# Pairs of eight products: the lower right block summed in the fifth product's bank, with differences of activations, and a fifth raw weight tile

## The chip, the core and the metric

The kernel runs on one core of a Trainium2 chip. The metric is device time in microseconds (us), the median of the runs of one program. PE is TensorE (matmul), PEld its weight load, DVE is VectorE, ACT is ScalarE, POOL is GpSimd and SP is SyncE, which here only issues DMAs. Matmuls sum in PSUM, eight banks of 128 x 512 fp32; POOL and DMA work on SBUF.

## What is computed

A decoder trunk of two layers for 256 tokens of width 2048, in fp32. Layer 0 is a gated short convolution, layer 1 an attention without softmax; each is followed by a squared-ReLU MLP with 8192 hidden units. Every sub-layer has a norm before and after. The change is in the MLP, which runs twice:

```python
D_MODEL = 2048; SEQ = 256; D_FF = 4 * D_MODEL

def sq_relu_mlp(u, w_up, w_down):
    return jnp.square(jax.nn.relu(u @ w_up)) @ w_down
...
        u = rmsnorm(h, mlp_pre_g[i])
        h = h + rmsnorm(sq_relu_mlp(u, mlp_w_up[i], mlp_w_down[i]), mlp_post_g[i])
```

## The kernel before

**Precision.** PE multiplies fp32r. Every operand is split into a high part (rounded to fp32r, on ACT) and a low part (the rest, on DVE); a product is three matmuls, high x high, high x low and low x high. Weights come by DMA from SP (`load_one`, L139) into one of `RAW` = 4 raw tiles of 128 x 1024, are split into `whi` (ACT, L163) and `wlo` (DVE, L174), and wait in a ring of 7 split tiles. A raw tile is free for the next load when it has been split.

**The MLP's steps.** The hidden units are cut into 8 steps of 1024, eight up tiles of 128 each. In step e the kernel makes the up tiles of step e+1 (`whole_up`, L944) and uses those of step e for the down projection, in turn: one up tile, then one *pair* (`Down.pair`, L1008), which multiplies two hidden tiles (256 hidden units) by a 256 x 1024 block of the down weights. Four pairs (m = 0 to 3) make one half h of a step, and one half gives one band j of 1024 output columns. `step_chunks` fixes the order of the weights, and PE's order is written out by hand (`manual_schedule` for PE, L89); DVE's, ACT's, POOL's and SP's order in this part is set by the scheduler, with `high_priority` where the code says so.

**An up tile** is 16 matmuls of 128 x 512 (high weights with both parts of the input) and 16 of 128 x 256 (low weights), all in bank 2 (`UP_BANK`). `finish` (L915) has ACT copy the bank's right half (`half`, L917), `Hidden.tile` (L857) has DVE add the left half to it (`s`, L859). After these two the bank is free. ACT applies ReLU and square, and the result is split into the parts of `hid`.

**A pair of seven products** (m = 1, 2, 3 in all steps but the last) is one level of Strassen-Winograd: the 256 x 256 activations and the 256 x 1024 weights are cut into 2 x 2 blocks, and seven block products, 21 matmuls, do instead of eight. Sums and differences of weights are made in `split_seven` (L191, `sums`), those of activations in `sums_of` (L873, `sq`). Products 1, 5, 6 and 7 have banks 6, 7, 0 and 1, tile `more` in the profile; three others go to banks 3, 4 and 5, tile `acc`. All are summed over a *plan* of eight pairs, the second half of one step and the first half of the next with the same band.

**A pair of eight products** (m = 0, and the last step's m = 1 to 3) is the plain block product, 24 matmuls (`eight`, L1036). The upper blocks go to banks 3 and 4, the lower left to bank 5. The lower right has no bank of its own in a plan: it is summed in bank 2 (`own == at`), and is added to its result at once (`add`, L951; DVE at L958, or an ACT copy at L956 the first time).

**At a plan's end** banks 3, 4 and 5 are added to their results, and `add_later` (L962), the *combine*, has ACT copy products 1, 6, 5 and 7 into the buffer `more`; nine accumulating DMAs from POOL (L921) then add them to the four results in SBUF, the last of them chained behind one another. In the last step `add_now` does this on DVE.

So per MLP there are 14 pairs of eight in bank 2's rotation and 42 of seven, the last of them behind the last up tile.

Of the kernel before, what the change touches and what calls it, by code (L numbers as in the profile page):

```python
# [9 lines left out]
F32 = mybir.dt.float32  # L10
# [18 lines left out]
LEAD_UP = 6  # L29
ALONE = 8  # L30
RING = 7
RAW = 4
AHEAD = 4
CALM = 12
UNIT = 1.36
# [51 lines left out]
def trunk(ctx, tc, x, xT, vecs, rows, ws, out):  # L87
# [740 lines left out]
    def result():  # L828
        return res.tile([P, 512], F32, tag="mg", name="mg")[:]
# [4 lines left out]
    def mlp(pool, i, before, after):  # L834
# [5 lines left out]
        def two_parts(parts, src):  # L840
            hi, lo = parts
            nc.scalar.activation(hi, src, AF.Copy)
            nc.vector.tensor_tensor(lo, src, hi.bitcast(F32), op=ALU.subtract)

        class Hidden:


            def __init__(self, e):
                self.xs, self.sums = [None] * (NF // 4), {}
                first, second = SEVEN[e]  # L850
                self.pairs = [2 * m for m in first]
                self.apart = [2 * m for m in first if m not in second]

            def x(self, n, b):
                return [part_of(self.xs, n, b, j) for j in range(2)]

            def tile(self, n, ps, half):  # L857
                s = pool.tile([P, T], F32, tag="s", name="s", bufs=3)
                nc.vector.tensor_tensor(s[:], ps[:, :T], half[:], op=ALU.add)  # L859
# [12 lines left out]

            def sums_of(self, n, x, y):  # L873

# [76 lines left out]
        def add(j, b, c, ps, last=False):  # L951
            r = part[b][2 * j + c]
            with tc.high_priority():
                if r is None:
                    r = part[b][2 * j + c] = result()
                    nc.scalar.activation(r, ps[:], AF.Copy)  # L956
                else:
                    nc.vector.tensor_tensor(r, r, ps[:], op=ALU.add)  # L958
            if last:
                after.post(b, 2 * j + c, r, r, scale[b][:])  # L960

        def add_later(j, p1, p5, p6, p7):  # L962
            t = pool.tile([P, 4, 512], F32, tag="gpost", name="more", bufs=1)
            t1, t5, t6, t7 = (t[:, m, :] for m in range(4))
            for to, ps in ((t1, p1), (t6, p6), (t5, p5), (t7, p7)):
                nc.scalar.activation(to, ps[:], AF.Copy)
            r = {(b, c): part[b][2 * j + c] for b in range(NB) for c in range(2)}
            adds.extend((
                (t6, t1), (r[0, 0], t1), (r[0, 1], t5), (r[1, 0], t7), (r[1, 1], t5),
                (r[0, 1], t6), (r[1, 0], t6), (r[1, 1], t7), (r[1, 1], t6),  # L970
            ))

        def add_now(j, p1, p5, p6, p7):
# [11 lines left out]
        class Down:  # L985


            def __init__(self, j, plan):
                self.j, self.plan, self.ps = j, plan, {}
                sevens_at = [at for at in plan if at[1] in SEVEN[at[0]][at[2]]]  # L990
                whole_at = [at for at in plan if at not in sevens_at and at[0] == STEPS - 1]
                self.range = {at: (at, at) for at in plan if at not in sevens_at}
                for own, ats in (("sum", plan), ("more", sevens_at), ("whole", whole_at)):
                    if ats:
                        self.range[own] = ats[0], ats[-1]

            def products(self, key, own, at, factors):

# [9 lines left out]
            def pair(self, at, first, xs):  # L1008
                e, m, _ = at
                seven = m in SEVEN[e][at[2]]  # L1010
                (self.seven if seven else self.eight)(at, first, xs, 2 * m)
                if "more" in self.range and at == self.range["more"][1]:
                    ps = [self.ps.pop(n) for n in (1, 5, 6, 7)]
                    self.combine = lambda: (add_now if at[0] == STEPS - 1 else add_later)(self.j, *ps)
                    if at != self.plan[-1]:
                        self.combine()
                        self.combine = None
                if at == self.plan[-1]:
                    last = e == STEPS - 1
                    for b, c in sorted(self.ps):  # L1020
                        add(self.j, b, c, self.ps.pop((b, c)), last)
                    if self.combine:
                        self.combine()

            def seven(self, at, first, xs, n):
                b11, b21, b22, t1, t2, t3, t4 = chunk(first)
                s1, s2, s3, s4 = xs.sums[n]
                for key, own, x, w in (
                    (1, "more", xs.x(n, 0), b11), ((0, 0), "sum", xs.x(n + 1, 0), b21), ((0, 1), "sum", s4, b22),
                    (5, "more", s1, t1), (6, "more", s2, t2), (7, "more", s3, t3),  # L1030
                    ((1, 0), "sum", xs.x(n + 1, 1), t4),
                ):
                    self.products(key, own, at, [(x, w)])
                spent(3.5 * UNIT)

            def eight(self, at, first, xs, n):  # L1036
                ws = [chunk(first + t) for t in range(2)]

                def factors(b, c, t):
                    return xs.x(n + t, b), [w[:, c * HALF : (c + 1) * HALF] for w in ws[t]]  # L1040
# [316 lines left out]
```

## Time and profile before

| | us |
|---|---|
| runs | 2152.21, 2153.68, 2164.34; median 2153.68 |
| the profiled execution | 2151.56, of which the span is 2149.4 |
| busy in the span | PE 2121.2, PEld 1804.9, DVE 1708.3, ACT 1386.8, POOL 116.2 |
| granted TensorE clock, mean | 0.997 |
| DMA | 450.28 MB, mean 209 GB/s |

How to read the views: a row of the timeline has start, duration, engine, line, operation, output <- inputs, shape and count, and in brackets the idle time before it and who ended that. A row of the waits has who waited, at which line, for whom, and then total us, times and the longest. A group's row has busy us and mean ns, then idle us before it. Numbers of buffers are left out of names. Ends of matmuls are modelled, since matmuls are pipelined.

### The profile page before, as it was taken

To read this page: it belongs to the slowest core of one execution; us is meant where nothing else is said; L and a number is where in the kernel's file an instruction comes from. 1 tells how busy PE (TensorE), PEld (TensorE's weight loads), DVE (VectorE), ACT (ScalarE), POOL (GpSimd) and SP (SyncE) were. 2 spreads that over 40 slices of the span, in tenths; PEclk is the share of its full clock that TensorE was granted. 3 is DMA by queue.
4 is the path that set the end of the run, shared out by engine and by line. 5 is a ranking of instruction groups with operands and counts; after the bars stand their busy time and mean duration, and the time that the engine had idled before them with its cause. 6 is when DMAs were issued, how large, how long until landed. Compare 5 with 4: busy or idle time off the path is not lost.

```text
span 2149.4 us, 29843 instructions
## 1 busy us (share of the span) xinstructions
PE 2121.2 (99%) x10816; PEld 1804.9 (84%) x10816; DVE 1708.3 (79%) x2525; ACT 1386.8 (65%) x2108; POOL 116.2 (5%) x139
## 2 busy tenths in 40 slices
PE   9999999999999999999999999999999999999998
PEld 8888888888888888888888888889888888888886
DVE  8766655888889888898866777558897888898987
ACT  7545444766666666676567888547666666666664
POOL 0000000010110100101000000000101001011010
PEclk9999999999999999999999999999999999999999
DMA  8655674586876867868574455645867678687684
GB/s 306 214 189 185 192 233 141 196 237 200 248 217 210 236 218 224 239 207 259 170 224 163 157 157 183 211 155 186 230 209 226 213 224 235 204 253 216 206 260 146
DMA packets 132917, 450.28 MB, mean 209 GB/s; under 512 B 14881, under 2 KB 15137, under 8 KB 131745
## 3 DMA queue, kind: packets, MB, share of 16 engines
q1 hardware_dynamic: 113472, 408.65, 58.0%
q0 software_dynamic: 19008, 39.33, 9.4%
q8 instruction: 85, 1.39, 0.3%
q14 instruction: 64, 0.52, 0.1%
q10 hardware_dynamic: 288, 0.39, 0.1%
HBM read 413.19 MB, written 2.10 MB: 193 GB/s over the span
## 4 chain that ended last, share of the span: by engine, by line
PE 84%; DVE 8%; DMA 5%; issue 2%; ACT 1%; SPq 0%; DVEq 0%; ACTq 0%
PE up L905 17%; PE acc L719 11%; PE up L912 9%; PE acc L300 7%; PE acc L301 7%; PE acc L302 7%; DMA raw<-w_mlp 5%; PE more L1004 4%; PE more L1005 3%; PE more L1006 3%; PE acc L1004 3%; PE acc L1005 3%; PE acc L1006 3%; DVE wlo L174 2%; DVE sums L200 2%
## 5 line engine op out<-in xcount | busy, mean ns | idle before, releaser
L174 DVE TENSOR_TENSOR wlo<-raw,whi 128x1024 fp32r<-128x1024 f32 (+1 forms) x506 | 605.4, 1208 | 200.7 <-ACT whi L163 142.8
L163 ACT ACTIVATE whi<-raw 128x1024 fp32r<-128x1024 f32 (+1 forms) x506 | 526.1, 1047 | 243.9 <-PE acc L302 79.7
L905 PE MATMUL up<-u,whi 128*128 128x512 f32 x1952 | 466.8, 390 | 4.7 <-DVE mg L958 4.1
L905 PEld LDWEIGHTS up<-u,whi 128*128 128x128 f32 x1952 | 364.7, 188 | 83.7 <-DVE mg L958 7.5
L912 PEld LDWEIGHTS up<-u,wlo 128*128 128x128 f32 x2048 | 263.6, 191 | 10.3
L912 PE MATMUL up<-u,wlo 128*128 128x256 f32 x2048 | 268.0, 283 | 0.0
L921 POOL DMA_DIRECT2D mg<-more x112 | 100.5, 997 | 1310.6 <-ACT s L860 573.8
L176 DVE SCALAR_TENSOR_TENSOR wlo<-raw,gv,whi 128x512 fp32r<-128x512 f32 (+1 forms) x160 | 132.0, 853 | 42.0 <-ACT whi L163 41.0
L719 PE MATMUL acc<-u,whi 128*128 128x512 f32 x672 | 156.5, 390 | 0.0
L163 ACT ACTIVATE whi<-raw,gv 128x512 fp32r<-128x512 f32 (+1 forms) x160 | 121.8, 801 | 50.7 <-PE acc L302 38.1
L300 PE MATMUL acc<-whi,u 128*128 128x512 f32 x384 | 153.1, 399 | 0.3 <-ACT tk L1194 0.3
L302 PE MATMUL acc<-whi,u 128*128 128x512 f32 x384 | 149.9, 390 | 0.0
L301 PE MATMUL acc<-wlo,u 128*128 128x512 f32 x384 | 149.7, 390 | 0.0
L719 PEld LDWEIGHTS acc<-u,whi 128*128 128x128 f32 x672 | 124.8, 188 | 25.0
L200 DVE TENSOR_TENSOR sums<-raw,sums 128x512 f32<-128x512 f32 x172 | 117.9, 685 | 1.4
L860 ACT ACTIVATE s<-s 128x256 f32<-128x256 f32 x128 | 51.9, 412 | 73.5 <-DVE s L859 72.9
L200 DVE TENSOR_TENSOR sums<-raw,raw 128x512 f32<-128x512 f32 x86 | 59.2, 689 | 48.1 <-DMA raw<-w_mlp 47.5
L917 ACT ACTIVATE half<-up 128x256 f32<-128x256 f32 x128 | 47.5, 378 | 75.4 <-PE up L912 75.3
L302 PEld LDWEIGHTS acc<-whi,u 128*128 128x128 f32 x384 | 72.1, 188 | 15.5
L719 PEld LDWEIGHTS acc<-u,wlo 128*128 128x128 f32 x672 | 83.5, 192 | 1.7
L719 PE MATMUL acc<-u,wlo 128*128 128x256 f32 x672 | 84.2, 283 | 0.0
L300 PEld LDWEIGHTS acc<-whi,u 128*128 128x128 f32 x384 | 72.2, 188 | 14.0 <-ACT tk L1194 0.7
(4467 smaller groups left out, 4073.1 us busy)
## 6 DMA issues: line engine op xcount, KB each, us to landing
raw<-w_mlp SPq DMA_DIRECT2D x512, 512.0 KB, 4.5
raw<-w_in SPq DMA_DIRECT2D x94, 512.0 KB, 4.0
mg<-more POOLq DMA_DIRECT2D x112, 256.0 KB, 7.2
raw<-w_out SPq DMA_DIRECT2D x32, 512.0 KB, 4.2
raw<-w_v SPq DMA_DIRECT2D x32, 512.0 KB, 4.4
raw<-w_k SPq DMA_DIRECT2D x32, 512.0 KB, 4.4
raw<-w_q SPq DMA_DIRECT2D x32, 512.0 KB, 4.3
raw<-w_wo SPq DMA_DIRECT2D x32, 512.0 KB, 3.6
```

The source lines that it names most:

```text
L163: rounded = nc.scalar.activation(hi[:, at], raw[i][:, at], AF.Copy, scale=1.0 if gain is None else gain)
L174: nc.vector.tensor_tensor(lo[:, at], t[:, at], hi[:, at].bitcast(F32), op=ALU.subtract)
L176: nc.vector.scalar_tensor_tensor(lo[:, at], t[:, at], gain, hi[:, at].bitcast(F32), op0=ALU.mult, op1=ALU.subtract)
L200: nc.vector.tensor_tensor(t, x, y, op=ALU.subtract)
L300: nc.tensor.matmul(ps[:], xh, hi[:, a], start=i == 0 and k == 0, stop=False)
L301: nc.tensor.matmul(ps[:], xh, lo[:, a], start=False, stop=False)
L302: nc.tensor.matmul(ps[:], xl, hi[:, a], start=False, stop=i == self.n - 1 and k == self.ks - 1)
L719: nc.tensor.matmul(ps[:, :cols], w, xs[:, :cols], start=k == 0 and part == parts[0], stop=k == KD - 1 and part == parts[1], skip_group_che ...
L905: nc.tensor.matmul(ps, weight(0, first, m), x, start=k == 0, stop=False)
L912: nc.tensor.matmul(pss[n][:, :T], weight(1, first, m), x, start=False, stop=k == KD - 1)
L1004: nc.tensor.matmul(self.ps[key][:], xh, hi, start=first, stop=False)
L1005: nc.tensor.matmul(self.ps[key][:], xh, lo, start=False, stop=False)
```

## The change

- *Lower right block of an eight.* Outside the last step it is summed in product 5's bank (7), whose range over the plan is now called `"fifth"` and begins at the eight. Product 5 is added to both right-hand results at the combine, so the upper right block would get it too; its bank therefore takes (upper - lower activations) x weights instead of upper activations x weights. `Hidden.tile` makes these differences (`dif`, one subtraction on DVE, then a high and a low part) for the two tiles of the coming step's m = 0. The block's own addition to its result is gone, and bank 2 is used by up tiles alone until the last step.
- *Order in an eight*: upper left, lower left, upper right, lower right. Before: upper left, upper right, lower right, lower left.
- *Combine.* Product 5 is copied first. Where the lower right result does not exist yet (the first plan of a band), ACT copies product 5 to it, and one accumulating DMA falls away (4 in the program). The DMAs stand in another order.
- `half` and `s` of every up tile get high priority.
- `RAW` = 5 instead of 4; the DMA scratch of the program is 8192 bytes instead of the default.

```diff
-RAW = 4
+RAW = 5
...
+                self.eights = [2 * m for m in range(4) if m not in first] if e < STEPS - 1 else []
...
-                nc.vector.tensor_tensor(s[:], ps[:, :T], half[:], op=ALU.add)
+                with tc.high_priority():
+                    nc.vector.tensor_tensor(s[:], ps[:, :T], half[:], op=ALU.add)
...
+                elif n - n % 2 in self.eights:
+                    if n % 2 == 0:
+                        self.sums[n] = pool.tile([P, 2, 2, P], F32R, tag="d", name="sums", bufs=2)
+                    parts = [self.sums[n - n % 2][:, n % 2, j, :] for j in range(2)]
+                    d = pool.tile([P, P], F32, tag="dif", name="dif", bufs=1)
+                    nc.vector.tensor_tensor(d[:], s[:, :P], s[:, P:], op=ALU.subtract)
+                    two_parts(parts, d[:])
...
-            copied = nc.scalar.activation(half[:], ps[:, T:], AF.Copy)
+            with tc.high_priority():
+                copied = nc.scalar.activation(half[:], ps[:, T:], AF.Copy)
...
-            for to, ps in ((t1, p1), (t6, p6), (t5, p5), (t7, p7)):
+            evicted = [(t5, p5), (t1, p1), (t6, p6), (t7, p7)]
+            r = {(b, c): part[b][2 * j + c] for b in range(NB) for c in range(2)}
+            if r[1, 1] is None:
+                r[1, 1] = part[1][2 * j + 1] = result()
+                evicted.insert(1, (r[1, 1], p5))
+            else:
+                adds.append((r[1, 1], t5))
+            for to, ps in evicted:
                 nc.scalar.activation(to, ps[:], AF.Copy)
...
-                if "more" in self.range and at == self.range["more"][1]:
+                if at == self.range["fifth"][1]:
...
-                    (5, "more", s1, t1), (6, "more", s2, t2), (7, "more", s3, t3),
+                    (5, "fifth", s1, t1), (6, "more", s2, t2), (7, "more", s3, t3),
...
-                own = "whole" if at[0] == STEPS - 1 else at
-                for c in range(2):
-                    self.products((0, c), "sum", at, [factors(0, c, t) for t in range(2)])
-                self.products((1, 1), own, at, [factors(1, 1, t) for t in range(2)])
-                if own == at:
-                    add(self.j, 1, 1, self.ps.pop((1, 1)))
-                self.products((1, 0), "sum", at, [factors(1, 0, t) for t in range(2)])
+                products((0, 0), "sum", lambda t: xs.x(n + t, 0), 0)
+                products((1, 0), "sum", lambda t: xs.x(n + t, 1), 0)
+                if at[0] == STEPS - 1:
+                    products((0, 1), "sum", lambda t: xs.x(n + t, 0), 1)
+                    products((1, 1), "whole", lambda t: xs.x(n + t, 1), 1)
+                else:
+                    products((0, 1), "sum", lambda t: [xs.sums[n][:, t, j, :] for j in range(2)], 1)
+                    products(5, "fifth", lambda t: xs.x(n + t, 1), 1)
...
-    nc = _bacc.Bacc("TRN2", target_bir_lowering=False, num_devices=1)
+    nc = _bacc.Bacc("TRN2", target_bir_lowering=False, num_devices=1, dynamic_dma_scratch_size=8192)
```

Three places in the order of the instructions. PE, the second half of the eight at step 0, half 1 (numbers are those of buffers and of weight tiles), before:

```order
L1004 MATMUL more_4559<-whi162_4419,hid4_3860 128x512
L1005 MATMUL more_4559<-wlo162_4420,hid4_3860 128x512
L1006 MATMUL more_4559<-whi162_4419,hid4_3860 128x512
L1004 MATMUL more_4559<-whi163_4458,hid4_3860 128x512
L1005 MATMUL more_4559<-wlo163_4459,hid4_3860 128x512
L1006 MATMUL more_4559<-whi163_4458,hid4_3860 128x512
L1004 MATMUL acc_4568<-whi162_4419,hid4_3860 128x512
```

After:

```order
L1023 MATMUL acc_4576<-whi163_4475,sums_3863 128x512
L1021 MATMUL more_4583<-whi162_4434,hid4_3860 128x512
L1022 MATMUL more_4583<-wlo162_4435,hid4_3860 128x512
L1023 MATMUL more_4583<-whi162_4434,hid4_3860 128x512
L1021 MATMUL more_4583<-whi163_4475,hid4_3860 128x512
L1022 MATMUL more_4583<-wlo163_4476,hid4_3860 128x512
L1023 MATMUL more_4583<-whi163_4475,hid4_3860 128x512
L914 MATMUL up_4590<-u4_3406,whi164_4481 128x512 x4
```

The lower right block (`more`) has moved from the third place to the last and into product 5's bank, and the upper right block reads the differences (`sums`).

DVE around the read-out of an up tile (`s`) ahead of an eight behind a combine (step 1, half 1; whi198 and wlo198 belong to the next seven), before:

```order
L174 TENSOR_TENSOR wlo198a_5362<-raw198_5259,whi198a_5361 128x512
L859 TENSOR_TENSOR s_5346<-up_5293,half_5344 128x256
L174 TENSOR_TENSOR wlo198b_5366<-raw199_5298,whi198b_5365 128x1024
L174 TENSOR_TENSOR wlo198t_5370<-sums_5356,whi198t_5369 128x1024
L843 TENSOR_TENSOR hid4_5350<-s_5346,hid4_5350 128x128
L882 TENSOR_TENSOR sq_5463<-s_5346 128x128
L958 TENSOR_TENSOR mg_4145<-mg_4145,more_5395 128x512
L174 TENSOR_TENSOR wlo198u_5374<-sums_5356,whi198u_5373 128x1024
```

After:

```order
L174 TENSOR_TENSOR wlo198a_5384<-raw198_5279,whi198a_5383 128x512
L861 TENSOR_TENSOR s_5368<-up_5315,half_5366 128x256
L174 TENSOR_TENSOR wlo198b_5388<-raw199_5320,whi198b_5387 128x1024
L174 TENSOR_TENSOR wlo198t_5392<-sums_5378,whi198t_5391 128x1024
L843 TENSOR_TENSOR hid4_5372<-s_5368,hid4_5372 128x128
L891 TENSOR_TENSOR sq_5484<-s_5368 128x128
L174 TENSOR_TENSOR wlo198u_5396<-sums_5378,whi198u_5395 128x1024
```

`s` stands between the same two rows; the addition of the block (`mg`) is gone.

ACT at the same place, before:

```order
L208 ACTIVATE whi198a_5361<-raw198_5259 128x512
L208 ACTIVATE whi198b_5365<-raw199_5298 128x1024
L208 ACTIVATE whi198t_5369<-sums_5356 128x1024
L917 ACTIVATE half_5344<-up_5293 128x256
L860 ACTIVATE s_5346<-s_5346 128x256
```

After:

```order
L208 ACTIVATE whi198a_5383<-raw198_5279 128x512
L208 ACTIVATE whi198b_5387<-raw199_5320 128x1024
L927 ACTIVATE half_5366<-up_5315 128x256
L208 ACTIVATE whi198t_5391<-sums_5378 128x1024
L862 ACTIVATE s_5368<-s_5368 128x256
```

`half` stands one weight split earlier.

More of the change, by code (lines that the diff above doesn't have):

```diff
@@ L964, in add_later @@
             t1, t5, t6, t7 = (t[:, m, :] for m in range(4))
-            for to, ps in ((t1, p1), (t6, p6), (t5, p5), (t7, p7)):
+            evicted = [(t5, p5), (t1, p1), (t6, p6), (t7, p7)]
[6 more added lines that the diff above has]
+            for to, ps in evicted:
                 nc.scalar.activation(to, ps[:], AF.Copy)
-            r = {(b, c): part[b][2 * j + c] for b in range(NB) for c in range(2)}
             adds.extend((
-                (t6, t1), (r[0, 0], t1), (r[0, 1], t5), (r[1, 0], t7), (r[1, 1], t5),
-                (r[0, 1], t6), (r[1, 0], t6), (r[1, 1], t7), (r[1, 1], t6),
+                (t6, t1), (r[0, 0], t1), (r[0, 1], t5), (r[1, 0], t7),
+                (r[1, 1], t7), (r[0, 1], t6), (r[1, 0], t6), (r[1, 1], t6),
             ))
@@ L991, in __init__ @@
                 whole_at = [at for at in plan if at not in sevens_at and at[0] == STEPS - 1]
[L992 to L995, printed above, removed]
+                fifth_at = [at for at in plan if at not in whole_at]
+                self.range = {
+                    own: (ats[0], ats[-1])
+                    for own, ats in (("sum", plan), ("more", sevens_at), ("fifth", fifth_at), ("whole", whole_at)) if ats
+                }
             def products(self, key, own, at, factors):
@@ L1037, in eight, with products @@
                 ws = [chunk(first + t) for t in range(2)]
-                def factors(b, c, t):
-                    return xs.x(n + t, b), [w[:, c * HALF : (c + 1) * HALF] for w in ws[t]]
-                own = "whole" if at[0] == STEPS - 1 else at
-                for c in range(2):
-                    self.products((0, c), "sum", at, [factors(0, c, t) for t in range(2)])
-                self.products((1, 1), own, at, [factors(1, 1, t) for t in range(2)])
-                if own == at:
-                    add(self.j, 1, 1, self.ps.pop((1, 1)))
-                self.products((1, 0), "sum", at, [factors(1, 0, t) for t in range(2)])
+                def products(key, own, x, c):
+                    self.products(key, own, at, [
+                        (x(t), [w[:, c * HALF : (c + 1) * HALF] for w in ws[t]]) for t in range(2)
+                    ])
+                products((0, 0), "sum", lambda t: xs.x(n + t, 0), 0)
[6 more added lines that the diff above has]
+                    products(5, "fifth", lambda t: xs.x(n + t, 1), 1)
                 spent(4 * UNIT)
```

## The prediction

> **What bounds the kernel now.** I read the page first, then who waits for whom on PE, then PE's timeline, then DVE's, and the DMA share last.
>
> ```profile
> span 2149.4 us, 29843 instructions
> PE 2121.2 (99%) x10816; PEld 1804.9 (84%) x10816; DVE 1708.3 (79%) x2525; ACT 1386.8 (65%) x2108; POOL 116.2 (5%) x139
> ```
>
> PE sets the time. But 99% is no proof that only 28 us are to be had: a matmul's row lasts 0.39 us while the next starts 0.23 us later (timeline below), so a row's modelled end hides part of each stall. Who PE waits for, first the matmuls and then the weight loads ahead of them:
>
> ```profile
> PE more L1004 <- DVE s L859: 12.9, 12, 2.2
> PE up L905 <- DVE mg L958: 4.1, 7, 0.7
> PE up L905 <- DVE s L859: 0.6, 1, 0.6
> ...
> PEld more L1004 <- DVE s L859: 21.8, 23, 2.7
> PEld up L905 <- DVE mg L958: 7.5, 8, 1.1
> ```
>
> Almost all of PE's waiting in 2.1 ms belongs to one bank, number 2. An up tile is summed in it and read out by DVE (`s`, L859). The eight's lower right block then uses the same bank ("more", L1004) after only 12 matmuls of cover, and the next up tile must wait until DVE has added that block to its result (`mg`, L958). No row has PE waiting for weights in the MLPs.
>
> An eight without a wait, then a seven, in PE's timeline (start, duration):
>
> ```profile
> 501.87 2.08 PE L912 MATMUL up<-u,wlo 128*128 128x256 f32 x16
> 503.79 0.40 PE L1004 MATMUL acc<-whi,hid 128*128 128x512 f32 x1
> 504.02 0.40 PE L1005 MATMUL acc<-wlo,hid 128*128 128x512 f32 x1
> ...
> 509.25 3.79 PE L905 MATMUL up<-u,whi 128*128 128x512 f32 x16
> 512.88 2.08 PE L912 MATMUL up<-u,wlo 128*128 128x256 f32 x16
> ...
> 519.58 3.79 PE L905 MATMUL up<-u,whi 128*128 128x512 f32 x16
> 523.21 2.08 PE L912 MATMUL up<-u,wlo 128*128 128x256 f32 x16
> ```
>
> From one up tile's end to the next one's, an eight takes 514.96 - 503.95 = 11.01 us and a seven 525.29 - 514.96 = 10.33. From an up tile's end to the next one's start there are 509.25 - 503.95 = 5.30 us in an eight (24 matmuls), 519.58 - 514.96 = 4.62 in a seven (21). The worst eight:
>
> ```profile
> 455.73 2.08 PE L912 MATMUL up<-u,wlo 128*128 128x256 f32 x16
> ...
> 460.17 0.39 PE L1006 MATMUL acc<-whi,hid 128*128 128x512 f32 x1
> 462.79 0.50 PE L1004 MATMUL more<-whi,hid 128*128 128x512 f32 x1 [2.23 <-DVE s L859]
> ...
> 464.05 0.62 PE L1006 MATMUL more<-whi,hid 128*128 128x512 f32 x1
> 464.47 0.63 PE L1004 MATMUL acc<-whi,hid 128*128 128x512 f32 x1
> ...
> 467.03 4.02 PE L905 MATMUL up<-u,whi 128*128 128x512 f32 x16
> 470.89 2.08 PE L912 MATMUL up<-u,wlo 128*128 128x256 f32 x16
> ```
>
> The up tile ended at 457.81, the next began at 467.03: 9.22 us, 3.92 over the clean 5.30. All waits together are taken from the ends of the first and last up tiles of each MLP's steps:
>
> ```profile
> 413.83 1.96 PE L912 MATMUL up<-u,wlo 128*128 128x256 f32 x15
> ...
> 1004.80 2.08 PE L912 MATMUL up<-u,wlo 128*128 128x256 f32 x16
> ...
> 1497.80 1.72 PE L912 MATMUL up<-u,wlo 128*128 128x256 f32 x13
> ...
> 2091.40 2.08 PE L912 MATMUL up<-u,wlo 128*128 128x256 f32 x16
> ```
>
> 415.79 to 1006.88 and 1499.52 to 2093.48 are 591.09 + 593.96 = 1185.05 us for 28 eights and 82 sevens. Without a wait they would take 28 x 11.01 + 82 x 10.33 = 1155.34. So **29.7 us** are lost: more than the 17.6 of PE's own wait rows, and what the weight loads' rows (29.3) say.
>
> **The change part by part.** *The bank.* The lower right block goes to product 5's bank 7, as the last product. The next reader of bank 2 is then the next up tile, 24 matmuls after the last one. `s` must end within 5.30 us of its up tile's end instead of 2.6, and the wait for `mg` has nothing left to wait for. The latest `s` of any eight is the one above, on DVE:
>
> ```profile
> 457.63 0.69 DVE L200 TENSOR_TENSOR sums<-raw,raw 128x512 f32<-128x512 f32 x1 [2.78 <-DMA raw<-w_mlp]
> ...
> 462.32 0.41 DVE L859 TENSOR_TENSOR s<-up,half 128x256 f32<-128x256 f32 x1
> ...
> 471.67 0.69 DVE L200 TENSOR_TENSOR sums<-raw,raw 128x512 f32<-128x512 f32 x1 [1.48 <-DMA raw<-w_mlp]
> ...
> 474.74 0.42 DVE L859 TENSOR_TENSOR s<-up,half 128x256 f32<-128x256 f32 x1
> ```
>
> It ended at 462.73, 4.92 us after the tile. That is inside 5.30, so with `s` where it is, every eight's wait goes. Only one seven waits now for more than 0.3 us, 0.6 us by the row above. Taken off: 29.7.
>
> *The clock.* Behind two waits like this PE also ran slower (a stretch, its length, each engine's busy time, then granted clock, DMA share, GB/s):
>
> ```profile
> 464.00:466.00 2.00, 2.00 (x6) 1.57 (x6) 1.41 (x3) 0.61 (x2) 0.87 (x1) 0.51 1.01 275
> ```
>
> The granted clock was 0.51, and from 464.05 matmuls came 0.42 us apart instead of 0.23, about 8 of them: 1.6 us each time, inside the 29.7. I take it to go with the wait. The Trainium skill (TensorE: Matmul & The Clock Gate, "HAM oscillation — how this bites in real kernels") gives as its abstract rule that idle gaps over about 3.4 us bring the half clock. By it a 2.23 us gap could not be the cause, the slow stretch would stay, and the sum would be 3.2 us smaller. The trace has the half clock begin 1.3 us after the gap's end, so I go by the row.
>
> *What is late next.* In the eights just behind a combine (one in each step) `s` is late because DVE stands in `sums` until a raw tile lands. If DVE and DMA do not move, PE arrives earlier and waits at the following seven. In the case above the next tile ended at 472.97 and its `s` at 475.16, 2.19 later. With the tile 3.92 earlier this is 6.11 against a cover of 4.62: 1.5 us given back. The same reckoning at all 28 eights gives more than 0.2 us at four, 1.5, 1.5, 2.0 and 3.0, in all **8.2 us** as the upper bound; the lower is 0. The fifth raw tile works against it: SP issues the same loads in the same order, but each is released one tile sooner, and DVE's idle rows of 2.78 and 1.48 us are the room. Whether it lands sooner is the question, as the engines are full there:
>
> ```profile
> 548.00:550.00 2.00, 1.11 (x6) 0.60 (x5) 2.00 (x4) 0.42 (x1) 1.63 (x2) 1.00 1.14 283
> ```
>
> A load that was requested before the burst of accumulating DMAs need not land inside it, so I lean to the rows with room: 2 us given back.
>
> *Differences of activations.* Added: 28 subtractions and 28 low parts on DVE, 28 roundings on ACT. Removed: 24 DVE additions of the block; four copies on ACT move from the eight to the combine.
>
> ```profile
> L843 DVE TENSOR_TENSOR hid<-s,hid x42: 278/283/293, 408.4 to 2005.8; 128x128 fp32r<-128x128 f32 x42
> L842 ACT ACTIVATE hid<-s x42: 289/295/315, 407.6 to 2003.8; 128x128 fp32r<-128x128 f32 x42
> ...
> L958 DVE TENSOR_TENSOR mg<-mg,more x26: 676/686/689, 508.1 to 2118.5; 128x512 f32<-128x512 f32 x26
> ...
> 420.00:1007.00 587.00, 579.25 (x2941) 491.73 (x2940) 512.38 (x721) 395.56 (x594) 55.97 (x64) 1.00 0.76 226
> ```
>
> DVE: 56 x 0.283 - 24 x 0.686 = -0.6 us. ACT: 28 x 0.295 = 8.3 us over two MLPs, beside 191 us idle in each. Cost on the path 0; the cover is DVE's 75 idle us in each MLP's steps. The differences are made a step ahead of their use.
>
> *Order of the products, banks.* The second product now uses bank 5, emptied last at the end of a plan, and the last one bank 7, emptied by a copy to `more`. On ACT, at the plan's end before the worst eight:
>
> ```profile
> 452.49 0.62 ACT L956 ACTIVATE mg<-acc 128x512 f32<-128x512 f32 x1
> ...
> 453.58 0.63 ACT L966 ACTIVATE more<-more 128x512 f32<-128x512 f32 x1
> ```
>
> Both are free by 454.21. The second product of that eight starts 6 matmuls after 457.6 and the fourth at about 461.7: 4.8 and 7 us of room, cost 0.
>
> *Raised priority* of `half` and `s`. On DVE the order keeps `s` between the same weight rows; on ACT `half` moves ahead of one split. Between -1 and +1 us; I take 0.
>
> *Half the DMA scratch, four accumulating DMAs fewer.* The trace shows no ring. Accumulations land in 7.2 us:
>
> ```profile
> mg<-more POOLq DMA_DIRECT2D x112, 256.0 KB, 7.2
> ```
>
> Their results are read a step, about 83 us, later. Between -0.5 us and the whole of that room; cost 0, since few can be in flight at a time.
>
> **Sum.** 29.7 - 2.0 = 27.7 us. The profiled execution took 2151.56 us (span 2149.4 and 2.2 around it), giving 2123.9. It lies 2.1 under the median of the three runs, 2153.68; for medians I forecast 2153.7 - 27.7 = **2126.0**. One per cent, about what a measurement of this kernel can tell from no change, is 21.5 us.
>
> **Rivals.** *Given back in full.* 29.7 - 8.2 = 21.5, 2132. For it: DMA share 1.14 in the burst. Against it: those idle rows of DVE. Chance 0.13, half of it on each side of one per cent.
>
> *The stretch behind a combine is bound by DMA as a whole*, so that its waits merely move to the sevens: of the 28 eights, the 14 behind a combine hold about 20.6 of the 29.7, and 9 remain: 2145, no change. Against it: after the worst eight, the next `s` came 2.2 us after its tile, not 4.6, so the sevens have room. Chance 0.08.
>
> *Slower: DVE waits in front of* `s`. Raised priority can place `s` so early that DVE stands until `half` is there, with all weight work behind it. Now DVE spends nothing there:
>
> ```profile
> L859 DVE TENSOR_TENSOR s<-up,half 128x256 f32<-128x256 f32 x128 | 52.8, 416 | 0.0
> ```
>
> DVE's spare is about 75 us in 55 up tiles, 1.36 us each. Above that weights fall behind and PE waits: at 1.8 us it is 110 x 0.44 = 48 us, 2174. It decides at 1.36 + 27.7/110 = 1.6 us. Against it: the order has moved `s` by no row at an eight. Chance 0.05.
>
> That the bank wait stays, because `s` moves later by more than the added 2.7 us of cover: 0.02, same.
>
> **How the numbers follow.** My forecast 0.72; the rivals 0.13, 0.08, 0.05, 0.02. Faster by over 1%: 0.72 + half of 0.13 less a little for the forecast's own edge, 0.76. Slower: 0.05. Within: 0.19. The likeliest case alone, with 0 to 5 us given back and 2 us of scatter, spans 2120 to 2131; the range reaches to the first rival with 6 us over it, 2120 to 2138, and leaves out under 2 in 10.
>
> **What would show it.** The wait rows of PE for `s` at the "more" product and for `mg` at the up tile are gone; the summed waits of PE are under 5 us, what is left stands at sevens behind a combine and names `s`. No slice between the start and the end shows a clock under 1. DVE busy is the same within 5 us, ACT about 8 more. The distance from first to last up tile falls from 1185 to about 1157. Wrong would be: new waits of PE for whi, wlo or the sums, idle time in front of `s` on DVE, or POOL's accumulations stretching into the next combine.

## The result, and the profile after

The changed kernel took 2121.39 us (median of 4 runs, 2120.85 to 2121.52), the kernel before, run beside it, 2156.27 (4 runs, 2152.21 to 2164.34). The ratio is 0.9833, 95% interval 0.9802 to 0.9864: faster by 1.7%. The forecast was 2126.0 in a range from 2120 to 2138. The number holds; the experiments show that a good part of the reason given for it does not.

The profiled execution took 2121.52 us. The head of its page:

```profile
span 2119.8 us, 29868 instructions
PE 2109.0 (99%) x10816; PEld 1805.5 (85%) x10816; DVE 1700.5 (80%) x2557; ACT 1389.6 (66%) x2136; POOL 112.6 (5%) x135
...
PE 99%; DMA 0%; DVE 0%; ACT 0%; SPq 0%; issue 0%; DVEq 0%; ACTq 0%
```

The last line is the chain that ended last: PE alone. Before it read PE 84%, DVE 8%, DMA 5%. The span fell by 2149.4 - 2119.8 = 29.6 us. All that PE's matmuls still wait for in the whole program:

```profile
PE warm L709 <- DVE ones L104: 1.1, 1, 1.1
PE lead L719 <- ACT whi L163: 0.7, 1, 0.7
PE tr L253 <- DVE h L480: 0.3, 1, 0.3
```

Bank 2 is gone from the list. The place that was the worst eight, and the seven behind it, in PE's timeline after:

```profile
456.36 2.08 PE L921 MATMUL up<-u,wlo 128*128 128x256 f32 x16
...
463.74 3.79 PE L914 MATMUL up<-u,whi 128*128 128x512 f32 x16
467.37 2.08 PE L921 MATMUL up<-u,wlo 128*128 128x256 f32 x16
...
474.07 3.80 PE L914 MATMUL up<-u,whi 128*128 128x512 f32 x16
```

458.44 to 463.74 is 5.30 us and 469.45 to 474.07 is 4.62, the two clean distances; before, the eight took 9.22. The ends of the first and last up tiles of each MLP's steps:

```profile
414.38 2.08 PE L921 MATMUL up<-u,wlo 128*128 128x256 f32 x16
...
991.88 2.08 PE L921 MATMUL up<-u,wlo 128*128 128x256 f32 x16
...
1484.31 2.08 PE L921 MATMUL up<-u,wlo 128*128 128x256 f32 x16
...
2061.80 2.08 PE L921 MATMUL up<-u,wlo 128*128 128x256 f32 x16
```

416.46 to 993.96 and 1486.39 to 2063.88 are 577.50 + 577.49 = 1154.99 us, 30.1 less than the 1185.05 before and what 28 clean eights and 82 clean sevens take (1155.34). Nothing was given back. The rest of the program is the same within 0.7 us: 492.4 us between the two MLPs' steps (492.6 before), 55.9 behind them (55.9), 0.7 more ahead of them.

So the time came out of the stretch that the prediction named. But another row moved that the prediction's sum does not contain. DVE's wait for raw weight tiles, before and then after:

```profile
DVE sums L200 <- DMA raw<-w_mlp: 63.9, 61, 2.8
```

```profile
DVE sums L200 <- DMA raw<-w_mlp: 17.7, 23, 1.8
```

A change of a bank on PE does not make weights land sooner. This is where the study began.

### The profile page after: what moved, and what is told of

It reads as the page before. It is cut to its first block, busy times and chain, and to the rows that moved or that the text cites. A ratio compares the mean times of both kernels' runs of the same rounds, so it can differ in the third digit from the quotient of the medians.

```text
span 2119.8 us, 29868 instructions
## 1 busy us (share of the span) xinstructions
PE 2109.0 (99%) x10816; PEld 1805.5 (85%) x10816; DVE 1700.5 (80%) x2557; ACT 1389.6 (66%) x2136; POOL 112.6 (5%) x135
## 4 chain that ended last, share of the span: by engine, by line
PE 99%; DMA 0%; DVE 0%; ACT 0%; SPq 0%; issue 0%; DVEq 0%; ACTq 0%
PE up L914 21%; PE up L921 12%; PE acc L719 11%; PE acc L300 8%; PE acc L302 8%; PE acc L301 7%; PE acc L1021 5%; PE acc L1022 5%; PE acc L1023 5%; PE more L1022 4%; PE more L1021 4%; PE more L1023 4%; PE lead L719 1%; PE up L916 1%; PE tr L253 1%; DMA raw<-w_in 0%
## 5 line engine op out<-in xcount | busy, mean ns | idle before, releaser
L921 PEld LDWEIGHTS up<-u,wlo 128*128 128x128 f32 x2048 | 263.6, 191 | 10.3
L301 PEld LDWEIGHTS acc<-wlo,u 128*128 128x128 f32 x384 | 72.3, 188 | 13.4
```

Of the source, the lines that this page charges most:

```text
L301: nc.tensor.matmul(ps[:], xh, lo[:, a], start=False, stop=False)
L921: nc.tensor.matmul(pss[n][:, :T], weight(1, first, m), x, start=False, stop=k == KD - 1)
```

## The experiments

Theory: the gain is bank 2's turn, as predicted. Rival: it is the fifth raw tile, which takes away what makes `s` late. All twelve kernels stand against the kernel before on the same chip.

| run | what differs | us, median (range) | ratio, 95% | DVE's wait for raw tiles, us |
|---|---|---|---|---|
| bank_alone | after, four raw tiles, no priority | 2145.66 (2142.42-2148.11) | 0.9946, 0.9929-0.9964 | 80.1 |
| raw5_only | before, five raw tiles | 2123.28 (2122.63-2123.51) | 0.9843, 0.9829-0.9858 | 12.4 |
| scratch_only | before, half the scratch | 2160.19 (2154.44-2163.59) | 1.0002, 0.9991-1.0012 | 73.7 |
| prio_only | before, raised priority | 2157.94 (2151.39-2163.74) | 1.0002, 0.9988-1.0016 | 67.9 |
| order_only | before, block last | 2170.45 (2169.04-2173.42) | 1.0067, 1.0049-1.0085 | 67.5 |
| no_adds | before, no accumulating DMAs | 2125.42 (2124.56-2125.72) | 0.9850, 0.9835-0.9864 | 14.3 |
| raw5_prio | before, five tiles, priority | 2122.95 (2122.25-2124.49) | 0.9840, 0.9825-0.9855 | 10.7 |
| bank_noprio | after, no priority | 2120.71 (2120.54-2120.78) | 0.9828, 0.9812-0.9845 | 19.3 |
| raw6_only | before, six raw tiles | 2121.88 (2121.57-2122.38) | 0.9834, 0.9820-0.9849 | 3.0 |
| gated_adds | before, accumulations spread | 2161.74 (2158.80-2170.88) | 1.0020, 1.0005-1.0035 | 63.6 |
| bank_gated | bank_alone, accumulations spread | 2134.17 (2131.52-2136.74) | 0.9889, 0.9871-0.9907 | 70.8 |
| bank_late5 | bank_noprio, fifth tile held back at the start | 2120.67 (2120.40-2121.22) | 0.9827, 0.9811-0.9843 | 14.4 |

### The parts of the change, one at a time

**bank_alone** is the changed kernel, with its half scratch, without the fifth raw tile and without the priority:

```diff
-RAW = 5
+RAW = 4
...
-                with tc.high_priority():
-                    nc.vector.tensor_tensor(s[:], ps[:, :T], half[:], op=ALU.add)
+                nc.vector.tensor_tensor(s[:], ps[:, :T], half[:], op=ALU.add)
...
-            with tc.high_priority():
-                copied = nc.scalar.activation(half[:], ps[:, T:], AF.Copy)
+            copied = nc.scalar.activation(half[:], ps[:, T:], AF.Copy)
```

> The changed kernel with four raw tiles again and without the raised priority of half and s: the bank, the differences, the order in the eight and the halved scratch alone. Bank theory: the whole gain lies in taking the lower right block out of the up tiles' bank, so 2121 to 2132 us, the upper end if sevens behind a combine give back the 8.2 us that were reckoned. Rival (the fifth raw tile brings s forward and that is the gain): 2140 or more, with PE waiting for s at up tiles.

It gained 0.5%, not 1.7. All 28 eights are clean at 5.30 us, as the prediction had it. But the wait came back at four sevens. PE's timeline, the next up tile's start at each of them:

```profile
478.10 5.26 PE L913 MATMUL up<-u,whi 128*128 128x512 f32 x16 [3.04 <-DVE s L860]
...
567.45 6.57 PE L913 MATMUL up<-u,whi 128*128 128x512 f32 x16 [3.74 <-DVE s L860]
...
1559.85 5.43 PE L913 MATMUL up<-u,whi 128*128 128x512 f32 x16 [3.25 <-DVE s L860]
...
1648.92 5.27 PE L913 MATMUL up<-u,whi 128*128 128x512 f32 x16 [3.31 <-DVE s L860]
```

The brackets sum to 13.3 us. The groups of 16 matmuls behind them last 5.26 to 6.57 us instead of 3.79, 7.4 us more in all, since the clock is at half there (columns as in the prediction's stretch, the clock third from the end):

```profile
478.00:480.00 2.00, 1.90 (x5) 1.52 (x6) 2.00 (x4) 1.92 (x4) 0.00 (x0) 0.50 0.57 121
```

Together 20.7 us given back of 29.7 (21.5 by the ends of the first and last up tiles), where the prediction had put 8.2 as the upper bound. DVE at the first of the four shows why:

```profile
472.58 0.69 DVE L200 TENSOR_TENSOR sums<-raw 128x512 f32<-128x512 f32 x1 [2.80 <-DMA raw<-w_mlp]
474.56 0.69 DVE L200 TENSOR_TENSOR sums<-raw,raw 128x512 f32<-128x512 f32 x1 [1.28 <-DMA raw<-w_mlp]
...
477.63 0.42 DVE L860 TENSOR_TENSOR s<-up,half 128x256 f32<-128x256 f32 x1
```

The up tile ended at 470.28, its `s` at 478.05: 7.77 us, against 4.62 of cover. My bound had kept DVE where it was, with that `s` ending at 475.16. It was 2.9 us later than that, standing 4.1 us for two raw tiles where it had stood 1.5 for one. Why those tiles came later than in the kernel before is not settled: PE asks earlier, and the order of the copies and accumulations at a combine changed as well. In sum DVE waits 80.1 us, 63.6 to 73.7 in the kernels below that keep four tiles, the old products and the accumulating DMAs. Moving the bank changes who waits for the late `s`, not that it is late.

**raw5_only** is the kernel before with the fifth tile and the smaller scratch that makes room for it:

```diff
-RAW = 4
+RAW = 5
...
-    nc = _bacc.Bacc("TRN2", target_bir_lowering=False, num_devices=1)
+    nc = _bacc.Bacc("TRN2", target_bir_lowering=False, num_devices=1, dynamic_dma_scratch_size=8192)
```

> The kernel before with five raw tiles (and the halved scratch that makes room). Bank theory: bank 2 still changes hands twice in each eight; waits for s shrink by what DVE idles in front of raw tiles there, waits for mg stay at about 6 us: 2140 to 2154 us. Rival (raw tile): in the changed kernel s ends within 2.1 us of its tile at every eight, inside even the old cover of 2.6 us; if that is the raw tile's doing, the waits for s go here too and 2125 to 2133 us come out.

2123.28 us, 36.0 under the kernel before on its chip: one number gives what the whole change gave (34.9 against the runs beside it; the best version, below, 37.3), with bank 2 used as before and 12 matmuls of cover. DVE at the place of the worst eight (before: a wait of 2.78 us, then `s` at 462.32):

```profile
455.43 1.41 DVE L200 TENSOR_TENSOR sums<-raw,sums 128x512 f32<-128x512 f32 x2
...
460.76 0.42 DVE L859 TENSOR_TENSOR s<-up,half 128x256 f32<-128x256 f32 x1
```

From these sums to `s` DVE works without a wait, and `s` ends 2.7 us after its tile (456.36 + 2.08 in this kernel too) instead of 4.9. What is left of bank 2's waits in the whole program is on the weight loads:

```profile
PEld more L1004 <- DVE s L859: 1.7, 4, 0.5
```

The theory falls here. The bank was where the lateness showed, and the fifth tile takes the lateness away.

**scratch_only**, since every run with five tiles also has the smaller scratch:

```diff
-    nc = _bacc.Bacc("TRN2", target_bir_lowering=False, num_devices=1)
+    nc = _bacc.Bacc("TRN2", target_bir_lowering=False, num_devices=1, dynamic_dma_scratch_size=8192)
```

> The kernel before with the DMA scratch halved to 8192 bytes and nothing else: four raw tiles, the old products, no raised priority. The fifth raw tile needs this smaller scratch to fit, so every run with five tiles had both; this run has the scratch alone. Theory (the gain of the fifth raw tile is the tile's): no difference, 2156 us with a ratio of 0.998 to 1.002, DVE's wait for raw tiles of the MLPs 60 to 70 us, PE's matmul waits for bank 2 at the lower right block 10 to 20 us. Rival (the smaller scratch changes how accumulating DMAs and loads share the engines, and so makes part of the gain): under 2145 us, DVE's wait under 45 us. Slower by the scratch (too few places for nine accumulations in flight): over 2165 us, accumulations landing later than 7.2 us.

No difference, 1.0002, and the accumulations land as before, median 7.4 us (7.2). So raw5_only's gain is the tile's. DVE's wait of 73.7 us beside 63.9 in a kernel of the same time also says how far that row scatters with four tiles.

**prio_only** raises the priority in the kernel before:

```diff
-                nc.vector.tensor_tensor(s[:], ps[:, :T], half[:], op=ALU.add)
+                with tc.high_priority():
+                    nc.vector.tensor_tensor(s[:], ps[:, :T], half[:], op=ALU.add)
...
-            copied = nc.scalar.activation(half[:], ps[:, T:], AF.Copy)
+            with tc.high_priority():
+                copied = nc.scalar.activation(half[:], ps[:, T:], AF.Copy)
```

> The kernel before with high priority for half and s, nothing else. Bank theory: s stays behind the sums that wait for a raw tile, so little moves: 2146 to 2156 us. Rival (priority): s moves ahead of them, waits for s go: 2125 to 2135 us.

Nothing: 1.0002, and bank 2's waits are there as before (18.6 us of matmuls for `s`, 4.5 for `mg`).

**order_only** puts the lower right block last in each eight of the kernel before, still in bank 2:

```diff
+                self.products((1, 0), "sum", at, [factors(1, 0, t) for t in range(2)])
                 self.products((1, 1), own, at, [factors(1, 1, t) for t in range(2)])
                 if own == at:
                     add(self.j, 1, 1, self.ps.pop((1, 1)))
-                self.products((1, 0), "sum", at, [factors(1, 0, t) for t in range(2)])
```

> The kernel before with the lower right block as the last of the eight's products, still in bank 2. s then has 18 matmuls of cover, about 3.9 us, and only three eights have a later one: waits for s fall from some 22 us to under 3. But the block's addition has no cover: DVE's 0.68 us and what stands in front of it on DVE, 0.9 to 1.5 us at each of 28 eights, 25 to 42 us of waits for mg at the up tile. Bank theory (both hand-overs count): 2155 to 2172 us. Rival (only the lateness of s counts): 2130 to 2136 us.

Slower by 0.7%. PE's waits show the trade:

```profile
PE up L905 <- DVE mg L958: 24.7, 24, 2.0
...
PE more L1004 <- DVE s L859: 4.8, 5, 1.3
PE up L905 <- ACT mg L956: 3.9, 4, 1.0
```

The wait for `s` shrinks to 4.8 us, but the block's own addition now has no matmuls over it, and each of the 28 eights waits about one microsecond for it. The new order is good only together with the other bank.

### What makes the raw tiles late

**no_adds** leaves the accumulating DMAs out of the kernel before, so four products are missing from the results:

```diff
-            for a, more in adds[:3]:
-                with tc.issue_after(copied.ins):
-                    nc.gpsimd.dma_start(a, more, accum_op=ALU.add)
             del adds[:3]
```

> The kernel before with four raw tiles and all as it was, but the 126 accumulating DMAs behind the combines are left out, so products 1, 5, 6 and 7 are missing from the results of these plans; only its time is of interest. Raw-tile theory (a load that has to pass through the burst of accumulating DMAs lands too late, DVE stands in front of it, s comes late, PE waits for bank 2): DVE's wait of 64 us for raw tiles falls under 20, PE's waits under 5, 2120 to 2130 us. Rival (four raw tiles are too few at any time, burst or not): DVE's wait stays over 40 us and 2140 or more comes out.

2125.42 us, nearly what the fifth tile gives. The same two stretches behind the combine at 456 us, first without the accumulations:

```profile
456.00:458.00 2.00, 2.00 (x17) 1.96 (x16) 2.00 (x3) 2.00 (x4) 0.00 (x0) 1.00 0.00 0
458.00:460.00 2.00, 2.00 (x10) 1.63 (x10) 2.00 (x4) 0.73 (x2) 0.00 (x0) 1.00 0.44 49
```

and then in the kernel before:

```profile
456.00:458.00 2.00, 2.00 (x18) 1.96 (x17) 0.37 (x1) 0.94 (x3) 0.00 (x0) 1.00 1.10 215
458.00:460.00 2.00, 2.00 (x11) 1.63 (x10) 2.00 (x4) 1.73 (x3) 0.00 (x0) 1.00 1.14 205
```

The third pair is DVE's busy time, the last but one number the DMA share. Without accumulations the DMA engines have run out of free tiles to fill (share 0.00) and DVE works all the time. With them the engines are full, and DVE, which works in its order, stands in `sums` with `s` behind it: 0.37 us busy out of 2. The changed kernel in the same place:

```profile
456.00:458.00 2.00, 2.00 (x17) 1.92 (x16) 1.97 (x3) 2.00 (x4) 1.38 (x2) 1.00 1.13 221
458.00:460.00 2.00, 2.00 (x12) 1.70 (x11) 2.00 (x4) 1.92 (x3) 0.00 (x0) 1.00 1.12 202
```

Its DMA engines are as full (1.13, 1.12) and DVE does not wait, because the tiles that it needs were asked for earlier. A seven uses four tiles in 10.33 us, one each 2.58. So with four tiles a load has about 10.3 us from its buffer's release to the release of the next one in that place, with five 12.9 (an estimate from those rows). Loads land no faster with five: between 400 and 1010 us the median is 4.6 us against 4.5 and the longest 10.7 against 8.9. They start one tile sooner.

**raw6_only** goes one further:

```diff
-RAW = 4
+RAW = 6
...
-    nc = _bacc.Bacc("TRN2", target_bir_lowering=False, num_devices=1)
+    nc = _bacc.Bacc("TRN2", target_bir_lowering=False, num_devices=1, dynamic_dma_scratch_size=8192)
```

> The kernel before with six raw tiles. Raw-tile theory: with five, DVE waits 12 us for raw tiles and PE for 1.7 us in loading weights; the sixth can only take off what is left, at most 2 us, and starts one more load into the crowded beginning, where five already cost about 0.6 us: 2121.5 to 2124 us. If lateness of raw tiles still cost more than the waits show: under 2121.

```profile
DVE sums L200 <- DMA raw<-w_mlp: 3.0, 5, 0.8
```

DVE's wait goes from 12.4 us to 3.0, and the time by 1.4 us, from 2123.28 to 2121.88, though on another chip; in the traces the distance from first to last up tile goes from 1156.4 to 1156.0. Little more is to be had from tiles, since PE hardly waits.

**gated_adds** keeps four tiles and spreads a combine's accumulations: up to three are issued when each up tile has been read, by a small copy on POOL.

```diff
+            if adds:
+                gate = small("gate", bufs=2)
+                seen = nc.gpsimd.tensor_copy(gate[:], half[:, :1])
             for a, more in adds[:3]:
-                with tc.issue_after(copied.ins):
+                with tc.issue_after(seen.ins):
```

> The kernel before with four raw tiles and all accumulating DMAs kept, but three at a time: a one-column copy of half on POOL stands ahead of each three, so they wait for an up tile's end and come in three groups some 10 us apart instead of as fast as their chain allows. Raw-tile theory: the burst is what makes raw tiles late, so DVE's wait for them falls from 64 us to 15 to 40, and the time to 2121 to 2140 us. Rival (what counts is the accumulations' total traffic beside four tiles, not the burst): DVE's wait stays at 60 or more and 2148 to 2160 comes out.

No gain, 1.0020. At 456 us DVE is now busy for all of both stretches, but its waits in the program sum to 63.6 us as before, and PE's to this:

```profile
PE more L1007 <- DVE s L859: 20.2, 12, 2.4
...
PE up L905 <- DVE s L859: 5.2, 9, 1.2
```

The wait has moved to later tiles. So it is not the burst as such: beside four tiles the same accumulations cost as much when they are spread in this way. **bank_gated** does the same to bank_alone (with the same lines):

```diff
-RAW = 5
+RAW = 4
...
-                with tc.issue_after(copied.ins):
+                with tc.issue_after(seen.ins):
```

> The bank's change with four raw tiles and no raised priority (2145.7 before this), with the accumulating DMAs gated in the same way. Raw-tile theory: the four waits at sevens behind a combine go with the burst: 2120 to 2128 us. Rival: they stay, 2140 or more.

2134.17, between the two forecasts. That is 11.5 us better than bank_alone (on another chip), though DVE waits almost as long (70.8 us against 80.1). PE now has nine short waits and no slow clock:

```profile
PE up L913 <- DVE s L860: 7.2, 9, 1.5
```

Together with the longer cover the spread helps, because none of the waits gets long; the mean granted clock is 0.999, in bank_alone 0.995. Against gated_adds, on the same chip, the bank's change is worth 27.6 us here (2161.74 to 2134.17). That points to how the lateness is spread: the latest `s` ends 8.5 us after its up tile in bank_alone and 6.2 in bank_gated, where the cover of a seven is 4.62. Which of the delays the spread shortens was not tested further.

### What the bank and the priority add to five tiles

**raw5_prio** is raw5_only with the two lines of prio_only, and **bank_noprio** the changed kernel without them:

```diff
-RAW = 4
+RAW = 5
...
+                with tc.high_priority():
...
```

> The kernel before with five raw tiles and raised priority, without the bank's change. Five tiles alone gave 2123.3, the whole change 2121.4. If the bank makes these 1.9 us: 2122.5 to 2124. If the priority makes them: 2121.0 to 2121.8.

```diff
-                with tc.high_priority():
-                    nc.vector.tensor_tensor(s[:], ps[:, :T], half[:], op=ALU.add)
+                nc.vector.tensor_tensor(s[:], ps[:, :T], half[:], op=ALU.add)
...
```

> The changed kernel without the raised priority: five raw tiles and the bank. If the bank makes the last 1.9 us: 2121.0 to 2121.8. If the priority makes them: 2122.5 to 2124.

2122.95 and 2120.71, on one chip. Against raw5_only and the changed kernel, which were measured apart from them, the priority is worth 0.3 us in one pair and costs 0.7 in the other: nothing that can be told. The bank, beside five tiles, is worth 1.6 us with the priority (2122.95 to 2121.39) and 2.6 without (2123.28 to 2120.71). The ranges of the runs don't touch, but neither pair was measured side by side. The traces agree on a size: from first to last up tile raw5_only and raw5_prio take 1156.4 us, the changed kernel and bank_noprio 1155.0. So it is there, at about 1.4 us, under 0.1%.

**bank_late5** asks if a fifth load in the first microseconds costs anything; the fifth tile is held until the first weights are split:

```diff
+    spare = wpool.tile([P, CW], F32, tag="raw", name="spare")
...
+        if i == 0:
+            nc.vector.tensor_copy(spare[:, :1], lo[:, CW - 1 :].bitcast(F32))
```

> The changed kernel without raised priority (2120.7) whose fifth raw tile is held back at the start until the first weight tile has been split, as with four tiles, by one column copied into it on DVE. If the fifth tile's early load is what delays PE's first steps (PE reached the MLP's first eight 0.65 us later than before the change): 2119.8 to 2120.4 us. If not: 2120.5 to 2121.0.

2120.67 against 2120.71: no. In the traces the first up tile of the MLP's steps ends at 415.62 us, without the hold at 415.70. These two are the fastest versions measured, 0.03% under the changed kernel and measured apart from it, so not told apart from it.

## Why the prediction was right, and where it was wrong

*The bank.* The size was right in the traces: 29.7 us forecast for the waits, 30.1 measured from first to last up tile. The cause was not. "So with `s` where it is, every eight's wait goes" is what bank_alone shows, but beside five tiles the new bank is worth 1.6 to 2.6 us, and without them a net 0.5%. The same waits can be taken away from two sides, by more cover over a late `s` or by an earlier `s`; the sum counted them once and put them down to the first. The fifth tile does the second, for 28.7 of the 30.1 us in the traces (1185.05 to 1156.4). Whatever clears these waits ends near the same time, so neither the number nor the signs that the prediction had named could tell the cause: raw5_only too has PE's waits for bank 2 gone, but for the 1.7 us of weight loads, and a distance near 1157.

*The level.* By medians the change is worth 34.9 us, against 27.7 forecast. The execution of the kernel before that was profiled, 2151.56 us, was a fast one: the medians of that kernel lie at 2156.27 to 2159.33, and the traces of scratch_only and prio_only, kernels of the same time, lose 38.5 and 36.0 us between first and last up tile where this one loses 29.7. Of the 4.6 us between 2126.0 and 2121.39, 2.0 are the give-back that did not come, and 2.1 were added for a difference between execution and median that the changed kernel, free of the wait, does not have. Nothing hangs on it that the eight read as the worst, 9.22 us, has one of 9.29 beside it in the second MLP.

*What is late next* is the step that failed. It took 2.0 us, with 8.2 as the upper bound. In the changed kernel it is 0; without the fifth tile it is 20.7. Two things were wrong in it. The bound held DVE and DMA still while PE moved forward, but DVE's stand for raw tiles grew. And it left out the slow clock behind the waits, 7.4 of the 20.7 us, though the prediction had that cost in its own sum. The four sevens of bank_alone are the four that it had reckoned. The right question was in it, as "whether it lands sooner"; the answer, that the fifth tile decides the whole case, got 6 us of weight. DVE in the changed kernel shows how near it was at the seven of 469.45:

```profile
467.97 0.69 DVE L200 TENSOR_TENSOR sums<-raw 128x512 f32<-128x512 f32 x1 [1.26 <-DMA raw<-w_mlp]
470.34 0.69 DVE L200 TENSOR_TENSOR sums<-raw,raw 128x512 f32<-128x512 f32 x1 [1.68 <-DMA raw<-w_mlp]
...
473.41 0.42 DVE L861 TENSOR_TENSOR s<-up,half 128x256 f32<-128x256 f32 x1
```

`s` ended at 473.83, 4.38 us after its tile, with 4.62 of cover. The changed kernel clears its worst seven by 0.24 us.

*The clock* went with the waits, as said. The mean is 0.999 after and was 0.997; the stretch from 464 to 466 us, at 0.51 before, is at 1.00. The sign named for it, no slice of the page under 1, says nothing: every slice reads 9 tenths before and after.

*Differences of activations.* The rows hold: 28 subtractions and 28 low parts at 0.284 us are 16.0, the 24 additions gone were 16.4. The page's busy time of DVE fell by 7.8 us all the same, outside the 5 that I had allowed, and ACT's rose by 2.8 instead of 8. The page counts time in which two instructions overlap once, and the short ones start 0.20 us apart while lasting 0.28. Counted like this from the two traces, the new rows add 11.4 us and the additions gone take off 14.7, which is 3.3 of the 7.8. The other 4.5 us are older rows, the `sums` of raw tiles above all, that last as long as before and overlap more with those ahead of them. None of it lay on the path.

*Order of the products, banks:* cost 0, as forecast; PE waits for neither bank 5 nor 7. order_only shows what it would have cost without the other bank.

*Raised priority:* 0 taken, within 0.7 us of 0 measured. The slower rival's mechanism is in the trace, at 1.9 us over 128 tiles where it needed 1.6 us at each:

```profile
L861 DVE TENSOR_TENSOR s<-up,half 128x256 f32<-128x256 f32 x128 | 53.1, 416 | 1.9 <-ACT half L927 1.9
```

*Half the DMA scratch:* 0, as forecast (scratch_only). Accumulations land in 8.0 us instead of 7.2 in the changed kernel; nobody waits for them.

*The rivals.* "The stretch behind a combine is bound by DMA as a whole", with 0.08, said that 20.6 us would move to the sevens. In bank_alone 20.7 did, and it took 2145.66 where the rival said 2145. The agreement is partly luck. Of the 14 eights behind a combine, ten no longer have a wait; at the other four places 11.4 us of waits became 21.5 at the sevens behind them. Nor is the stretch bound by DMA as a whole: bank_gated moves the same bytes and is 11.5 us faster, and with a fifth tile PE waits for none of it. What the rival had right is that the worst waits pass on to the sevens when the cover alone grows. The argument against it, that the seven behind the worst eight had room, was read from a trace in which PE itself was late.

## What to carry to other kernels

When a wait is found at a buffer's turn, follow the late producer back to what it waited for, and price the cure there first: a longer cover can pass the worst of such waits on to the next place, as here from two dozen eights to four sevens. A change of several parts that could each remove the same wait needs a sum for each part alone, since the waits are there only once, and a sign that one part would show and the other not. And a bound that keeps the other engines still is not a bound where they share queues with the engine that moves; count load buffers by the time of one round (tiles times microseconds per tile) against a load's landing time in the busiest stretch, not against its median (from 400 to 1010 us: up to 8.9 us within the 10.3 of four tiles, which must hold the split as well, and up to 11.4 within the 12.9 of five; the medians are 4.5 and 4.7).

## What the runs showed of the hardware

- The scatter of the kernel before goes with its wait for raw tiles. With four tiles and accumulations the runs of a kernel lie up to 0.6% apart (2151.46 to 2160.52 of 13, 2152.21 to 2164.34 of 4); with five tiles, or without the accumulations, 0.01 to 0.1%.
- The length of a gap on PE does not alone decide whether the clock falls. Half clock came behind gaps of 3.04 to 3.74 us in bank_alone, of 2.23 us in the kernel before and of 2.05 us in gated_adds. It did not come behind one of 2.86 us in prio_only, nor behind this one in scratch_only, after which the clock stays at 1.00:

```profile
552.89 0.50 PE L1004 MATMUL more<-whi,hid 128*128 128x512 f32 x1 [2.42 <-DVE s L859]
```

```profile
553.00:555.00 2.00, 2.00 (x9) 1.65 (x10) 2.00 (x2) 1.01 (x3) 0.87 (x1) 1.00 0.90 231
```

The Trainium skill (TensorE: Matmul & The Clock Gate, "HAM oscillation — how this bites in real kernels") puts the limit for idle gaps at about 3.4 us; here gaps well below that brought half clock, though not every one, and the measurement decides. What fits the traces is where a gap lies. In each trace the stretches of half clock begin whole multiples of 3.413 us apart, as at 464.05 and 1634.82 in the kernel before, 343 of them. Cut each trace into pieces of that length from there, and sum PE's idle time in each piece, from 60 us after the start to the last matmul. In the seven traces with gaps over 1.1 us, half clock begins behind the 12 pieces with 2.01 us or more of idle time, and behind none with 1.94 or less (an inference from these traces alone, with the modelled ends of the matmuls).

- Full DMA engines (share 1.10 to 1.14) do not by themselves cost time: the changed kernel's are as full at the same place.
